# Contrast adjustment: rows of 48 KB in 4 buffers and 8 tiles in place of rows of 32 KB in 6 buffers and 12 tiles

## The chip, the cores and the metric

The kernel runs on one core of one Trainium2 chip. A core has a matrix engine (PE), a vector engine (DVE), a scalar engine (ACT), GpSimd (POOL) and SyncE (SP), 16 DMA engines that move data between HBM and the on-chip memory SBUF, and a small accumulation memory, PSUM, that PE writes. SBUF has 128 partitions; a tile is a block of all 128 partitions with so many elements in each. The metric is the device time of one execution, in microseconds (us).

## The reference

```python
def setup_inputs():
    batch, c, h, w = 16, 3, 512, 512
    return {
        "x": np.random.rand(batch, c, h, w).astype(np.float32),
        "factor": np.float32(1.5),
    }

def reference(x: np.ndarray, factor: np.float32) -> np.ndarray:
    mean = np.mean(x, axis=(2, 3), keepdims=True)
    return np.clip(mean + factor * (x - mean), 0, 1).astype(np.float32)
```

There are 48 images (batch times channel) of 262,144 pixels in float32. Each is read once, 50.33 MB in all, its mean is taken, and 1.5 times the pixel minus half the mean, cut to 0 and 1, is written, another 50.33 MB. A pixel can be written only when the whole of its image has been read.

## The kernel before

The input is seen as one flat row of numbers. A tile takes 128 rows of 8192 numbers (32 KB each, 4 MB together), one row for each partition. An image is 32 rows, so a tile holds four whole images, and each partition belongs to one image. There are 12 tiles.

The tiles pass through `ring` (L66), one SBUF tile of six slots; tile t uses slot t modulo 6. Everything is done in place in the slot. The instructions are issued in the order in which they are written out (the schedule is manual), so each engine's queue has them in this order; waits are put in from the data that they share.

- `load` (L68 to L76) issues on SP's queue. Tile 0 comes in two pieces, 2048 numbers of each row and then 6144; tile 1 alone; tiles 2 and 3 in one DMA, and tiles 4 and 5 in one, so that both tiles of a pair arrive together. The load of tile t + 6 is written after the compute of tile t, and waits for the store of tile t.
- `compute` (L78) sums each row. DVE takes 4352 of its numbers (L81), ACT the other 3840 with a copy whose sum is kept (L84; the copy goes into `junk` and is not used). Two matmuls with the constant matrix `blockw` (L86, L87) add the sums of the 32 partitions of each image and scale them, so that PSUM's `bias` holds the shift of its image for each partition.
- DVE then multiplies by the factor and adds the shift (L91) and clamps (L94), over the whole row at once; in tile 0 first over 2048 numbers and then over 6144.
- `store` (L100, L101) issues on ACT's queue after the clamp: tile 0 in two pieces, the others whole. So ACT's queue is: sum of tile t, store of tile t, sum of tile t + 1, and so on.

`blockw` is made by POOL at the start with five memsets (L61, L63).

Of the kernel before, what the change touches and what calls it, by code (L numbers as in the profile page):

```python
# [1 line left out]

# [4 lines left out]


P = 128  # L10
ROW = 8192
BUFS = 6
SHORT = 2048
FIRST = (SHORT, ROW - SHORT)
SUM = 4352


@with_exitstack
def kernel(
    ctx: ExitStack,  # L20
    tc: tile.TileContext,
    x: bass.AP,
    factor: float,
    out: bass.AP,
):

    nc = tc.nc
    f32 = mybir.dt.float32  # L30
    Alu = mybir.AluOpType
    Act = mybir.ActivationFunctionType

    B, C, H, W = x.shape
    n_img, n_pix = B * C, H * W
    ppi = n_pix // ROW
    per_tile = P // ppi
    n_tiles = n_img // per_tile
    assert ppi * ROW == n_pix and per_tile * n_tiles == n_img

    factor = float(factor)
    wconst = (1.0 - factor) / float(n_pix)

    x_f = x.rearrange("b c h w -> (b c h w)")
    out_f = out.rearrange("b c h w -> (b c h w)")

    def dram(ap, t, c0=0, c1=ROW):
        return bass.AP(tensor=ap.tensor, offset=t * P * ROW + c0, ap=[[ROW, P], [1, c1 - c0]])

    consts = ctx.enter_context(tc.tile_pool(name="consts", bufs=1))  # L50
    xpool = ctx.enter_context(tc.tile_pool(name="xpool", bufs=1))
    small = ctx.enter_context(tc.tile_pool(name="small", bufs=1))
    psum = ctx.enter_context(tc.tile_pool(name="psum", bufs=1, space=bass.MemoryType.PSUM))


    sums = small.tile([P, 2 * n_tiles], f32, name="sums")
    junk = small.tile([P, ROW - SUM], f32, name="junk")
    bias = psum.tile([P, n_tiles], f32, name="bias")

    blockw = consts.tile([P, P], f32, name="blockw")  # L60
    nc.gpsimd.memset(blockw, 0.0)  # L61
    for a in range(0, P, ppi):
        nc.gpsimd.memset(blockw[a : a + ppi, a : a + ppi], wconst)  # L63


    ring = xpool.tile([P, BUFS, ROW], f32, name="ring")  # L66

    def load(t, c0=0, c1=ROW, n=1):  # L68

        b = t % BUFS  # L70
        src = bass.AP(
            tensor=x_f.tensor,
            offset=t * P * ROW + c0,
            ap=[[ROW, P], [P * ROW, n], [1, c1 - c0]],
        )
        nc.sync.dma_start(out=ring[:, b : b + n, c0:c1], in_=src)  # L76

    def compute(t):  # L78
        xt = ring[:, t % BUFS, :]
        own = sums[:, 2 * t : 2 * t + 2]  # L80
        nc.vector.tensor_reduce(  # L81
            out=own[:, 0:1], in_=xt[:, 0:SUM], axis=mybir.AxisListType.X, op=Alu.add
        )
        nc.scalar.activation(out=junk, in_=xt[:, SUM:ROW], func=Act.Copy, accum_out=own[:, 1:2])  # L84
        shift = bias[:, t : t + 1]
        nc.tensor.matmul(shift, blockw, own[:, 1:2], start=True, stop=False)  # L86
        nc.tensor.matmul(shift, blockw, own[:, 0:1], start=False, stop=True)  # L87
        c = 0
        for n in FIRST if t == 0 else [ROW]:
            part = xt[:, c : c + n]  # L90
            nc.vector.tensor_scalar(  # L91
                out=part, in0=part, scalar1=factor, scalar2=shift, op0=Alu.mult, op1=Alu.add
            )
            nc.vector.tensor_scalar(  # L94
                out=part, in0=part, scalar1=0.0, scalar2=1.0, op0=Alu.max, op1=Alu.min
            )
            store(t, c, c + n)
            c += n

    def store(t, c0, c1):  # L100
        nc.scalar.dma_start(out=dram(out_f, t, c0, c1), in_=ring[:, t % BUFS, c0:c1])  # L101

    with tc.manual_schedule():
        load(0, c1=SHORT)
        load(0, c0=SHORT)
        load(1)
        load(2, n=2)
        load(4, n=2)
        for t in range(n_tiles):
            compute(t)  # L110
            if t + BUFS < n_tiles:
                load(t + BUFS)


# [1 line left out]
_INS = ['x', 'factor']  # L116
_OUTS = [((16, 3, 512, 512), 'float32')]

_NUMBERS = {'factor': 1.5}


# [26 lines left out]
```

## Time and profile before

| what | value |
|---|---|
| median of 4 runs | 239.38 us (239.18 to 239.67) |
| the profiled execution, whole | 239.2 us |
| its span, first to last instruction | 237.3 us |
| moved by DMA | 100.66 MB, 424 GB/s over the span |
| DVE busy | 163.1 us, 69% |
| ACT busy | 43.2 us, 18% |
| PE busy | 14.0 us, 6% |
| DMA packets | 3712 |

How to read it: the page describes one execution. The span is cut into 40 equal slices, each about 5.9 us; a digit in them is the busy share in tenths, and 9 is 90% or more. A line for a queue has its packets, its megabytes, and the time of its packets as a share of what 16 engines have in the span. A line for a group of instructions has the source line, engine, operation, output and inputs with their shapes (partitions x elements of each), how many there were, their busy time in us, the mean of one in ns, and then the idle time of the engine just before them with what ended most of it. A line of the timeline has the start in us, the duration in us, the engine, line and operation, and in brackets the idle time before it and what ended it. "ACTq" and "SPq" are the queues on which DMAs are issued; such a line tells of the issue, not of the transfer. Beside these views the trace has a record of each DMA packet: its queue, size, start and duration.

### The profile page before, as it was taken

The page shows a single profiled execution, that of the slowest core. Times are in us where ns is not written, and L with a number is a line of the kernel's source. Part 1 is how long each engine was busy: PE and PEld are TensorE (multiplying, and loading weights), DVE is VectorE, ACT ScalarE, POOL GpSimd, SP SyncE. Part 2 cuts the span into 40 slices and gives each one's busy share as a digit, 9 for nine tenths or more (in the row PEclk, how much of TensorE's full clock was granted, in tenths as well). Part 3 has the DMA queues.
Part 4 walks back from the last instruction along what each step waited for, and adds up shares of the span by engine and source line. Part 5 has one row for each costly group of instructions (what it writes and reads, how often), then busy time and mean ns, then how long its engine had stood idle before and what let it go on. Part 6 is the DMA issues. An engine that isn't in the chain of part 4 may idle for free.

```text
span 237.3 us, 285 instructions
## 1 busy us (share of the span) xinstructions
PE 14.0 (6%) x48; PEld 12.0 (5%) x48; DVE 163.1 (69%) x38; ACT 43.2 (18%) x25; POOL 0.9 (0%) x9
## 2 busy tenths in 40 slices
PE   0010010001010001010010100100100100010000
PEld 0010010001010001000010100100100100010000
DVE  0079989048989328998989898891892795687000
ACT  2050220041050023050320504101400500500000
POOL 1000000000000000000000000000000000000000
DMA  8999999999999999999999999999999999999996
GB/s 309 398 442 442 435 425 356 447 443 434 431 425 414 431 442 442 442 442 442 425 414 425 425 431 442 442 442 442 442 431 409 420 431 436 436 442 442 442 442 265
DMA packets 3712, 100.66 MB, mean 424 GB/s; under 512 B 384, under 2 KB 384, under 8 KB 384
## 3 DMA queue, kind: packets, MB, share of 16 engines
q1 hardware_dynamic: 1840, 50.33, 49.8%
q10 hardware_dynamic: 1872, 50.33, 49.1%
HBM read 50.33 MB, written 50.33 MB: 424 GB/s over the span
## 4 chain that ended last, share of the span: by engine, by line
DMA 57%; DVE 29%; another core or an unknown queue 3%; PE 1%; SPq 1%; issue 0%; DVEq 0%
DMA ring<-in_x_dram 41%; DMA out_dram<-ring 16%; DVE sums L81 10%; DVE ring L91 9%; DVE ring L94 9%; PE bias L87 1%; SPq L76 1%; DVEq L91 0%
## 5 line engine op out<-in xcount | busy, mean ns | idle before, releaser
L81 DVE TENSOR_REDUCE sums<-ring 128x1 f32<-128x4352 f32 x12 | 56.2, 4683 | 45.8 <-DMA ring<-in_x_dram 45.8
L84 ACT ACTIVATE junk<-ring 128x3840 f32<-128x3840 f32 x12 | 40.8, 3403 | 163.4 <-DMA ring<-in_x_dram 107.6
L91 DVE TENSOR_SCALAR ring<-ring,bias 128x8192 f32<-128x8192 f32 (+2 forms) x13 | 54.1, 4163 | 8.9 <-PE bias L87 7.4
L94 DVE TENSOR_SCALAR ring<-ring 128x8192 f32<-128x8192 f32 (+2 forms) x13 | 53.3, 4099 | 0.4
L86 PE MATMUL bias<-sums,blockw 128*128 128x1 f32 x24 | 7.0, 361 | 190.9 <-ACT junk L84 190.9
L86 PEld LDWEIGHTS bias<-sums,blockw 128*128 128x128 f32 x24 | 6.0, 311 | 191.8 <-ACT junk L84 175.5
L87 PE MATMUL bias<-sums,blockw 128*128 128x1 f32 x24 | 7.0, 362 | 4.3 <-DVE sums L81 3.9
L87 PEld LDWEIGHTS bias<-sums,blockw 128*128 128x128 f32 x24 | 6.0, 311 | 5.3 <-DVE sums L81 5.1
L84 ACT ACTIVATION_READ_ACCUMULATOR junk<-ring 128x1 f32 x12 | 2.2, 187 | 0.0
L84 ACT ACT_TABLE_LOAD x1 | 1.3, 1283 | 0.7 <-PEq L129 0.7
L63 POOL MEMSET blockw<- 32x32 f32 x4 | 0.5, 117 | 0.2
L61 POOL MEMSET blockw<- 128x128 f32 x1 | 0.2, 204 | 0.3 <-POOLq L129 0.3
L129 POOL MEMSET const-bfloat16-1.0<- 128x1 bf16 x1 | 0.1, 111 | 0.0
L129 POOL MEMSET const-uint8-127<- 128x1 uint8 x1 | 0.1, 111 | 0.0
L129 POOL MEMSET const-float32-1.0<- 128x1 f32 x1 | 0.1, 108 | 0.0
L129 POOL MEMSET const-float32-0.0<- 128x1 f32 x1 | 0.1, 103 | 0.2 <-issue 0.2
## 6 DMA issues: line engine op xcount, KB each, us to landing
out_dram<-ring ACTq DMA_DIRECT2D x11, 4096.0 KB, 36.0
ring<-in_x_dram SPq DMA_DIRECT2D x7, 4096.0 KB, 49.5
ring<-in_x_dram SPq DMA_DIRECT2D x2, 8192.0 KB, 66.8
ring<-in_x_dram SPq DMA_DIRECT2D x1, 3072.0 KB, 11.5
out_dram<-ring ACTq DMA_DIRECT2D x1, 3072.0 KB, 28.7
ring<-in_x_dram SPq DMA_DIRECT2D x1, 1024.0 KB, 4.6
out_dram<-ring ACTq DMA_DIRECT2D x1, 1024.0 KB, 18.5
```

Source lines behind the costliest of these rows:

```text
L61: nc.gpsimd.memset(blockw, 0.0)
L63: nc.gpsimd.memset(blockw[a : a + ppi, a : a + ppi], wconst)
L76: nc.sync.dma_start(out=ring[:, b : b + n, c0:c1], in_=src)
L81: nc.vector.tensor_reduce(out=own[:, 0:1], in_=xt[:, 0:SUM], axis=mybir.AxisListType.X, op=Alu.add)
L84: nc.scalar.activation(out=junk, in_=xt[:, SUM:ROW], func=Act.Copy, accum_out=own[:, 1:2])
L86: nc.tensor.matmul(shift, blockw, own[:, 1:2], start=True, stop=False)
L87: nc.tensor.matmul(shift, blockw, own[:, 0:1], start=False, stop=True)
L91: nc.vector.tensor_scalar(out=part, in0=part, scalar1=factor, scalar2=shift, op0=Alu.mult, op1=Alu.add)
L94: nc.vector.tensor_scalar(out=part, in0=part, scalar1=0.0, scalar2=1.0, op0=Alu.max, op1=Alu.min)
L129: nc = _bacc.Bacc("TRN2", target_bir_lowering=False, num_devices=1)
```

## The change

The rows become 12288 numbers, three parts of 4096 (48 KB), so a tile has 6 MB and six images, and there are 8 tiles. The ring has 4 slots in place of 6; it takes the same room. An image is 64 parts, which is 21 rows and a third, so image boundaries fall inside rows, at thirds: each row is in one image or in two, and its thirds have to be summed and shifted apart.

- `load` and `store` keep their queues. Tile 0 comes in with 2048 numbers of each row and then 10240; tile 1 alone; tiles 2 and 3 in one DMA; the others when their slot's store is done.
- Sums: DVE sums the first 6144 numbers as three halves of parts, in one instruction with three results (L129). ACT sums 2048 and then 4096 numbers, two copies written over their own input (L135). A row has five partial sums.
- POOL multiplies the five sums with `cls`, constant masks that say to which of three classes of images a third belongs, and gets 15 numbers (L136). One matmul with a new `blockw` adds them over the partitions (L142). DVE multiplies the result, three times over, with `pick`, constant masks again (L143), and reduces it to three shifts for each partition, one for each third (L149), which lie in SBUF.
- Shift: in tiles 1 to 6 DVE shifts the first third (L165) and ACT the other two (L155); in tiles 0 and 7 DVE takes two thirds and ACT one. The clamp is DVE's (L170), over the whole row of 12288; in tile 0 over 2048 and then 10240. It waits for DVE's and ACT's shifts.
- `of`, `cls`, `pick` and `blockw` are made by POOL at the start: two memsets, twelve affine selects, one addition and three copies; before the first select the program has the load of a POOL library.

On each queue the order is: SP has the loads only. ACT has, for a tile, its two sums, its shifts, the store. DVE has the reduce, the two small operations for the bias, its shifts, the clamp. POOL has its setup, and then one multiplication for each tile.

```diff
-ROW = 8192
-BUFS = 6
-SHORT = 2048
-FIRST = (SHORT, ROW - SHORT)
-SUM = 4352
+PART = 4096
+ROW = 3 * PART
+HALF = PART // 2
+BUFS = 4
+FIRST = (HALF, ROW - HALF)
+HEAD = (HALF, ROW - HALF)
+IMGS = 6
+CLS = 3
+NSUM = 5
...
+    of = consts.tile([P, IMGS, NSUM], f32, name="of")
+    pool.memset(of, 1.0)
...
+    cls = consts.tile([P, CLS, NSUM], f32, name="cls")
+    pool.tensor_tensor(out=cls, in0=of[:, 0:CLS], in1=of[:, CLS:IMGS], op=Alu.add)
+    pick = consts.tile([P, 3, CLS, NSUM], f32, name="pick")
+    for k in range(3):
+        pool.tensor_copy(
+            out=pick[:, k], in_=cls[:, :, 2 * k : 2 * k + 1].to_broadcast([P, CLS, NSUM])
+        )
...
-    nc.gpsimd.memset(blockw, 0.0)
-    for a in range(0, P, ppi):
-        nc.gpsimd.memset(blockw[a : a + ppi, a : a + ppi], wconst)
+    pool.memset(blockw, wconst)
...
+    while p0 < period:
...
+        pool.affine_select(
+            out=cols, in_=cols, pattern=[[-3 * period, P // period], [0, p1 - p0]],
+            compare_op=Alu.is_ge, fill=0.0, base=2 - units * first, channel_multiplier=3,
+        )
+        pool.affine_select(
+            out=cols, in_=cols, pattern=[[3 * period, P // period], [0, p1 - p0]],
+            compare_op=Alu.is_gt, fill=0.0, base=units * (last + 1), channel_multiplier=-3,
+        )
...
     def compute(t):
         xt = ring[:, t % BUFS, :]
-        own = sums[:, 2 * t : 2 * t + 2]
+        own = sums[:, t, :]
         nc.vector.tensor_reduce(
-            out=own[:, 0:1], in_=xt[:, 0:SUM], axis=mybir.AxisListType.X, op=Alu.add
-        )
-        nc.scalar.activation(out=junk, in_=xt[:, SUM:ROW], func=Act.Copy, accum_out=own[:, 1:2])
-        shift = bias[:, t : t + 1]
-        nc.tensor.matmul(shift, blockw, own[:, 1:2], start=True, stop=False)
-        nc.tensor.matmul(shift, blockw, own[:, 0:1], start=False, stop=True)
+            out=own[:, 0:3], in_=xt[:, 0 : 3 * HALF].rearrange("p (m c) -> p m c", m=3), axis=X,
+            op=Alu.add,
+        )
+        for m, a, b in (3, 3 * HALF, 4 * HALF), (4, 2 * PART, ROW):
+            part = xt[:, a:b]
+            nc.scalar.activation(out=part, in_=part, func=Act.Copy, accum_out=own[:, m : m + 1])
+        pool.tensor_tensor(
+            out=spread[:, t, :].rearrange("p (r m) -> p r m", r=CLS),
+            in0=own[:, None, :].to_broadcast([P, CLS, NSUM]),
+            in1=cls,
+            op=Alu.mult,
+        )
+        nc.tensor.matmul(totals[:, t, :], blockw, spread[:, t, :], start=True, stop=True)
+        nc.vector.tensor_tensor(
+            out=picked[:, t],
+            in0=totals[:, t, :][:, None, :].to_broadcast([P, 3, CLS * NSUM]),
+            in1=pick.rearrange("p k r m -> p k (r m)"),
+            op=Alu.mult,
+        )
+        nc.vector.tensor_reduce(out=bias[:, t, :], in_=picked[:, t], axis=X, op=Alu.add)
+        kd = 1 if 0 < t < n_tiles - 1 else 2
+        for k in range(kd, 3):
+            third = xt[:, k * PART : (k + 1) * PART]
+            nc.scalar.activation(
+                out=third, in_=third, func=Act.Identity, scale=factor, bias=bias[:, t, k : k + 1]
+            )
         c = 0
         for n in FIRST if t == 0 else [ROW]:
-            part = xt[:, c : c + n]
-            nc.vector.tensor_scalar(
-                out=part, in0=part, scalar1=factor, scalar2=shift, op0=Alu.mult, op1=Alu.add
-            )
+            end = c + n
+            for k in range(kd):
+                a, b = max(c, k * PART), min(end, (k + 1) * PART)
+                if a < b:
+                    part = xt[:, a:b]
+                    nc.vector.tensor_scalar(
+                        out=part, in0=part, scalar1=factor, scalar2=bias[:, t, k : k + 1],
+                        op0=Alu.mult, op1=Alu.add,
+                    )
+            part = xt[:, c:end]
             nc.vector.tensor_scalar(
                 out=part, in0=part, scalar1=0.0, scalar2=1.0, op0=Alu.max, op1=Alu.min
             )
-            store(t, c, c + n)
+            store(t, c, end)
+            c = end
...
-        load(0, c1=SHORT)
-        load(0, c0=SHORT)
+        c = 0
+        for n in HEAD:
+            load(0, c, c + n)
+            c += n
         load(1)
         load(2, n=2)
-        load(4, n=2)
         for t in range(n_tiles):
             compute(t)
             if t + BUFS < n_tiles:
                 load(t + BUFS)
```

## The prediction

> **What bounds the kernel now.** I read the slices of the span first, then the DMA queues, then the groups of instructions, and last the timeline around the last tile.
>
> ```profile
> DMA  8999999999999999999999999999999999999996
> GB/s 309 398 442 442 435 425 356 447 443 434 431 425 414 431 442 442 442 442 442 425 414 425 425 431 442 442 442 442 442 431 409 420 431 436 436 442 442 442 442 265
> DMA packets 3712, 100.66 MB, mean 424 GB/s; under 512 B 384, under 2 KB 384, under 8 KB 384
> q1 hardware_dynamic: 1840, 50.33, 49.8%
> q10 hardware_dynamic: 1872, 50.33, 49.1%
> ```
>
> The DMA engines are at 9 tenths or more from the second slice to the last but one, and the two queues' packets fill 49.8 + 49.1 = 98.9% of 16 engines' span, 234.7 of 237.3 us. The kernel is bound by DMA from end to end. 384 packets under 512 B are the completion writes: 16 for each of 24 DMAs. The other 3328 are rows, 208 on each engine.
>
> ```profile
> L81 DVE TENSOR_REDUCE sums<-ring 128x1 f32<-128x4352 f32 x12 | 56.2, 4683 | 45.8 <-DMA ring<-in_x_dram 45.8
> L84 ACT ACTIVATE junk<-ring 128x3840 f32<-128x3840 f32 x12 | 40.8, 3403 | 163.4 <-DMA ring<-in_x_dram 107.6
> L86 PE MATMUL bias<-sums,blockw 128*128 128x1 f32 x24 | 7.0, 361 | 190.9 <-ACT junk L84 190.9
> L84 ACT ACTIVATION_READ_ACCUMULATOR junk<-ring 128x1 f32 x12 | 2.2, 187 | 0.0
> L61 POOL MEMSET blockw<- 128x128 f32 x1 | 0.2, 204 | 0.3 <-POOLq L129 0.3
> ```
>
> These give the prices of compute. The idle time of DVE and ACT is put down to loads, that of PE to ACT's sums.
>
> ```profile
> 18.14 1.29 DVE L91 TENSOR_SCALAR ring<-ring,bias 128x2048 f32<-128x2048 f32 x1 [0.68 <-PE bias L87]
> 203.85 4.69 DVE L81 TENSOR_REDUCE sums<-ring 128x1 f32<-128x4352 f32 x1 [4.99 <-DMA ring<-in_x_dram]
> 209.27 4.49 DVE L91 TENSOR_SCALAR ring<-ring,bias 128x8192 f32<-128x8192 f32 x1 [0.74 <-PE bias L87]
> 213.80 4.43 DVE L94 TENSOR_SCALAR ring<-ring 128x8192 f32<-128x8192 f32 x1
> 218.26 0.34 ACTq L101 DMA_DIRECT2D out_dram<-ring  x1
> ```
>
> The last tile is in at 203.8 and its store is issued at 218.26. By the packet records of the trace the store ahead of it ends only at 226.5, and the last store's first packet starts at 225.9: the last tile's compute has 7.7 us to spare, and is no tail. So only two things can change the time: what the packets themselves cost, and whether DMA goes idle.
>
> **Part 1, the packets.** Bytes stay 100.66 MB. A packet is one row of one DMA. The packet records of undisturbed stores give 309 ns for 8 KB, 912 ns for 24 KB, 1213 ns for 32 KB: a line of 0.03678 ns per byte plus 8 ns per packet. Before, per engine and direction: 8 x 0.309 + 8 x 0.912 + 88 x 1.213 = 116.5 us, twice 233.0, and 24 completion writes of 9 ns, 0.2. The records run from 1.74 to 236.17 us, 234.4, so 1.2 us is lost: 0.8 in the first load (8 packets in 3.25 us for 2.47), 0.4 elsewhere. After: 8 tiles, the first in two pieces, give 8 packets of 8 KB, 8 of 40 KB at 1.514, 56 of 48 KB at 1.816, each extrapolated on the line: 116.3, twice 232.55, and 17 DMAs (8 loads, 9 stores) with 0.15. That is 0.55 us less; the 1.2 us lost stay, since the first piece is 8 KB a row again. Nothing in the trace is as long as 48 KB. Bounds: no saving per byte over the 32 KB row, 1.5 x 1.213 = 1.82, leaves 0.1 us of gain; if long loads go at the mean of all 32 KB loads, 1225 ns instead of 1213, the 56 loads cost 56 x 1.5 x 0.012 = 1.0 more, and the change loses 0.5. I take the line, because three sizes lie on it within 1 ns and most of the load excess stands between 21 and 40 us, when stores begin.
>
> The Trainium skill, "SBUF — State Buffer", section "The DMA setup-cost knee", gives every transfer some 2 us that don't scale with bytes and advises the largest single transfers. As a sum, 7 DMAs fewer would be 14 us of gain, some 225 us. The queue rows leave no place for it: 24 such costs are 48 us and 2.6 us of the span are without packets, since one queue moves data while the other's transfer completes.
>
> **Part 2, compute of a tile.** L81 is 4352 / 4.68; at 0.96 elements per ns and 0.15 fixed, 6144 elements take 6.55. ACT's sums: 3840 in 3.40 is 1.2 per ns and 0.2 fixed, so 2048 and 4096 take 1.9 + 3.6, and two accumulator reads 0.4: 5.9, beside DVE's 6.55 and shorter, so it hides there; were ACT held back, each 0.6 us beyond counts. Clamp and shift go by 0.521 ns per element plus 0.2 (1.29 for 2048, 4.49 for 8192): 4096 is 2.35, 12288 is 6.6. The bias: before, sums to shift is 0.75 (two passes of the second matmul, 0.6, and hops). After, a POOL multiply of 15 elements, the matmul, a DVE multiply of 45 and a DVE reduce to 3. No row shows such small ones; the nearest are POOL memsets of 0.1 to 0.2 and accumulator reads of 0.19. From 1.1 (each at 0.1) to 3 (POOL and both DVE operations at 0.5 and more); I take 1.5, near the memsets. The second matmul of a tile goes away, 0.6 us that was hidden beside DVE's reduce. That ACT's copies are written over the ring instead of junk, and that the shift reads its bias from SBUF, not PSUM, I cost at nothing: as many elements are written, and L91 with the PSUM operand takes 4.49 where L94 without takes 4.43. Then ACT shifts two thirds, 2 x 3.6 + 0.1 = 7.3, with DVE's one third (2.35) beside it, and the clamp 6.6 waits for ACT. DVE per middle tile: 6.55 + 1.5 + 7.3 + 6.6 = 22; the last tile, where DVE takes two thirds, 6.55 + 1.5 + 4.7 + 6.6 = 19.5. One tile's DMA, in and out, is 16 x 1.816 = 29.05, so compute is 76% of it (before 14.4 of 19.4, 74%). On ACT's queue the store stands behind the shifts and waits for the clamp, and the next tile's ACT sums stand behind the store; they begin with DVE's reduce, as before. SP's queue holds loads alone, each waiting for the store that frees its slot.
>
> **Part 3, does DMA go idle?** Tile 0: its rows end at 5.0 + 8 x 1.514 = 17.1, DVE starts 0.5 later as before, reduce to 24.2, bias at 25.7. ACT's third to 29.3 holds the first store to 29.4 (before 20.7); the second, after DVE's 1.2, 2.35 and a clamp of 5.5, goes at 37.3. Tile 1 is in by 32, its store goes at 59.3. Loads run alone until then, and are covered: the four slots hold 25.2 MB, as six did. Tiles 2 and 3 are one DMA and arrive together: 17.1 + 24 x 1.816 plus the store packets between them (8 x 0.309, some 7 x 1.514) is about 73. The second store ends near 75, and frees the slot of tile 4; the load queue is empty for some 4 us while the store queue runs alone. From 76.5 each load takes 29.05 beside a store: tile 6 is in at 164, tile 7 at 193. Compute follows: tile 2 from 73, 3 from 95, 4 from 117, 5 from 139, 6 on arrival, its store at 186; tile 7 to 193 + 19.5 = 212.5. DMA ends at 236.2 - 0.55 = 235.6, the last store takes 8 x 1.816 = 14.5 alone and must go by about 220. Spare: 7 us, nearly that of before. Nothing is late, so the path stays DMA and compute is costed at nothing: its cover is the store backlog.
>
> **Part 4, POOL's setup.** Before: 5 memsets on blockw, done by 1.6 us. After, 2 memsets, 12 affine selects in chains of two, one add, three copies, and a library load ahead of the selects. It is wanted at 24.2. Bounds from the memset rows: 18 x 0.2 = 3.6 us at the least; if each select were as slow as a 4683 ns reduce, 12 x 4.7 = 56. I take under 20 us, nearest to the memsets by size (42 columns or fewer). A delay X of tile 0 costs nothing at first: loads of 58 us and the first tile's stores of 14.6 us keep DMA busy to 74 while tile 1's store would go at 59.3 + X. Beyond X = 14, setup past 38 us, DMA stands still.
>
> The Trainium skill, "GPSIMD Engine Reference", section "Instruction dispatch", adds about 6 us for the first call of a freshly loaded library. With it the setup is 10 to 26 us, still inside the 38; no row before shows such a load.
>
> **The sum.** The profiled execution took 239.2 (span 237.3, 1.9 around it); less 0.55 is 238.65. The median of the four runs is 0.18 above the profiled one: 239.38 - 0.55 = 238.8.
>
> **Rivals.** A, compute becomes the bound and it is slower: tiles 2 to 7 run back to back from 73: 73 + 5 x 22 + 19.5 = 202.5 against 220, so 17.5 / 6 = 2.9 us more per tile is free; beyond it every 1 us per tile is 6 us of tail. At 26 us a tile (POOL hop and small DVE operations 5.5 instead of 1.5) it loses 6.6: 245. For it: four hops over three engines that no row prices; against: all small rows are near 0.2. B, the POOL setup comes after 38 us: at 44 DMA idles 6 us, 245. For it: twelve selects unknown; against: the small sizes. C, long rows do not pay: 0.1 of gain to 0.5 of loss, 239.3 to 239.9. For it: 8 ns a packet is all the gain there is; against: the line of three sizes.
>
> **How the numbers follow.** A measurement here can tell 0.2%, 0.48 us, from no change: the bar is 238.9. My case has 0.68 with 238.2 to 239.2; below, the other 0.4 us of loss and the 0.2 by which runs lay under their median also come off; above, half the gain stays. Of it 0.52 is faster, 0.16 the same. A has 0.10 and B 0.07, all slower. C has 0.15: 0.02 faster, 0.06 same, 0.07 slower. Sums: 0.54, 0.22, 0.24. The range takes C whole and the small end of A and B, to 241; some 0.15 lies above, 0.05 below.
>
> **What would show it.** 2576 packets, 272 of them small; 48 KB packets at 1816 ns (part 1; at 1820 and more C); DMA digits of 9 to the last slice; middle clamps of 6.6 starting 15.4 us after their reduce (part 2); the last store issued near 212 (part 3; past 220 is A); tile 0's matmul at 25 (part 4; past 39 is B). The forecast fails if the digits of DMA fall anywhere before the end, or if time around the span grows from 1.9, for instance with the library.

## The result, and the profile after

The changed kernel takes 239.65 us (median of 35 executions, 239.19 to 245.19) beside 239.26 us for the kernel before (54 executions, 238.97 to 239.91): a ratio of 1.0025, 95% interval 1.0014 to 1.0036. It is slower by a quarter of a per cent, where 0.25% faster was forecast. The ratio is one of means of fast executions: it leaves out the four from 244.6 to 245.2, as any that is more than 1.5% above the fastest of its kernel (their granted clock is 1.0 as in the others), and the median of the other 31 is 239.50. The shape of the numbers matters more than the median: 23 of the 35 are between 239.19 and 239.93, near the kernel before, and 12 are above 240. No execution of the kernel before is above 240. The execution profiled here took 240.18, with a span of 238.1.

The slices of the span and the DMA queues of the changed kernel:

```profile
DMA  7999989998999999999999999999999999999994
GB/s 286 440 462 396 454 376 447 462 383 388 484 410 427 405 512 405 396 479 446 396 396 520 405 396 471 454 396 396 520 396 405 471 447 396 405 512 405 405 446 215
DMA packets 2577, 100.67 MB, mean 423 GB/s; under 512 B 272, under 2 KB 272, under 8 KB 272
q1 hardware_dynamic: 1280, 50.33, 49.6%
q10 hardware_dynamic: 1296, 50.33, 48.8%
```

The packets are as counted in the prediction (2576 and one instruction fetch), and nowhere before the last slice does DMA stand still. The share of the packets, 98.4% of 238.1, is 234.3 us, 0.4 less than before. At the end only the last slice is different: 4 tenths where it was 6.

Its groups of instructions, and POOL's setup and the last tile in the timeline:

```profile
L129 DVE TENSOR_REDUCE sums<-ring 128x3 f32<-128x6144 f32 x8 | 52.4, 6550 | 45.8 <-DMA ring<-in_x_dram 45.8
L155 ACT ACTIVATE ring<-ring,bias 128x4096 f32<-128x4096 f32 x14 | 51.3, 3704 | 18.3 <-DVE bias L149 18.3
L143 DVE TENSOR_TENSOR picked<-totals,pick 128x45 f32<-128x45 f32 x8 | 1.6, 205 | 8.5 <-PE totals L142 8.5
L136 POOL TENSOR_TENSOR spread<-sums,cls 128x15 f32<-128x15 f32 x8 | 1.7, 214 | 198.6 <-DVE sums L129 198.6
L149 DVE TENSOR_REDUCE bias<-picked 128x3 f32<-128x45 f32 x8 | 1.6, 200 | 0.3
```

```profile
1.10 0.27 POOL L70 TENSOR_SCALAR_AFFINE_SELECT of<-of 128x30 f32<-128x30 f32 x1
3.55 0.47 POOL L81 COPY pick<-cls 128x15 f32<-128x15 f32 x3
...
204.13 0.21 POOL L136 TENSOR_TENSOR spread<-sums,cls 128x15 f32<-128x15 f32 x1 [29.23 <-DVE sums L129]
...
205.52 4.62 DVE L165 TENSOR_SCALAR ring<-ring,bias 128x4096 f32<-128x4096 f32 x2
...
210.24 6.56 DVE L170 TENSOR_SCALAR ring<-ring 128x12288 f32<-128x12288 f32 x1
216.83 0.34 ACTq L124 DMA_DIRECT2D out_dram<-ring  x1
```

Compute is what the prediction said it would be, each small operation 0.2 us, POOL ready at 4 us. The last store is issued at 216.8, and by the packet records its first packet starts at 221.1: 4.3 us to spare. So neither compute nor the setup is the answer, and the answer lies in the DMA packets.

**One account for all traces.** The packet records let the end of DMA be written as a sum, in us for one engine (the mean of 16): the start of the first packet, plus what the packets take by their sizes (8 ns each and 0.03678 ns per byte), plus what single packets took beyond that (held up), less the time in which the records of neighbouring packets overlap. To that comes how far the last of the 16 engines ends after their mean. The records do not name the engine; each DMA has 16 completion writes, one behind the last packet of each engine, and an engine's end is read from these. For the kernel before and for all traces of the changed kernel that follow:

| traced execution | time | first packet | by size | held up | overlap | mean end | last engine after the mean |
|---|---|---|---|---|---|---|---|
| before | 239.2 | 1.94 | 233.0 | 1.58 | 0.65 | 235.93 | 0.24 |
| after | 240.18 | 1.99 | 232.5 | 1.73 | 0.41 | 235.91 | 1.02 |
| after, second trace | 239.51 | 1.95 | 232.5 | 1.77 | 0.41 | 235.92 | 0.57 |
| after, third | 239.34 | 2.00 | 232.5 | 1.70 | 0.41 | 235.90 | 0.22 |
| after, fourth | 242.62 | 2.02 | 232.5 | 1.92 | 0.41 | 236.13 | 3.20 |
| after, fifth | 239.40 | 2.00 | 232.5 | 1.59 | 0.41 | 235.79 | 0.31 |
| after, sixth | 240.39 | 2.01 | 232.5 | 1.80 | 0.41 | 235.99 | 1.36 |
| after, seventh | 239.31 | 1.98 | 232.5 | 1.67 | 0.41 | 235.82 | 0.25 |

Each line closes to 0.1 us (232.5 is 232.55 rounded). Two things stand in it. The 0.5 us by size are there, but 0.24 of them come back because fewer packets overlap (0.65 over 208 packets and 0.41 over 144 are both some 3 ns each), and about 0.15 because more is held up (1.74 on the mean of the seven, 1.68 on that of the four quiet ones). The mean end moves by 0.15 us at most in the quiet executions. And the three traced executions above 240 are those in which one or two engines end late.

### The profile page after: what moved, and what is told of

The parts are those of the page before. It is cut to its first block, busy times and chain, and to the rows that moved or that the text cites. A ratio compares the mean times of both kernels' runs of the same rounds, so it can differ in the third digit from the quotient of the medians.

```text
span 238.1 us, 250 instructions
## 1 busy us (share of the span) xinstructions
PE 4.9 (2%) x16; PEld 4.0 (2%) x16; DVE 131.4 (55%) x44; ACT 97.4 (41%) x47; POOL 5.0 (2%) x30
## 4 chain that ended last, share of the span: by engine, by line
DMA 40%; DVE 32%; ACT 8%; another core or an unknown queue 7%; issue 2%; PE 1%; POOL 0%; SPq 0%; POOLq 0%; DVEq 0%; ACTq 0%
DMA ring<-in_x_dram 22%; DMA out_dram<-ring 17%; DVE ring L170 14%; DVE sums L129 14%; ACT ring L155 8%; DVE ring L165 4%; PE totals L142 1%; DVE picked L143 0%; DVE bias L149 0%; POOL spread L136 0%; SPq L120 0%; POOLq L217 0%; POOLq L136 0%; ACTq L155 0%
## 5 line engine op out<-in xcount | busy, mean ns | idle before, releaser
L135 ACT ACTIVATE ring<-ring 128x2048 f32<-128x2048 f32 (+1 forms) x16 | 44.1, 2756 | 92.8 <-DMA ring<-in_x_dram 63.4
L129 DVE TENSOR_REDUCE sums<-ring 128x3 f32<-128x6144 f32 x8 | 52.4, 6550 | 45.8 <-DMA ring<-in_x_dram 45.8
L170 DVE TENSOR_SCALAR ring<-ring 128x12288 f32<-128x12288 f32 (+2 forms) x9 | 52.6, 5849 | 30.5 <-ACT ring L155 30.3
L155 ACT ACTIVATE ring<-ring,bias 128x4096 f32<-128x4096 f32 x14 | 51.3, 3704 | 18.3 <-DVE bias L149 18.3
L165 DVE TENSOR_SCALAR ring<-ring,bias 128x4096 f32<-128x4096 f32 (+1 forms) x11 | 23.6, 2158 | 0.3
L142 PE MATMUL totals<-spread,blockw 128*128 128x15 f32 x16 | 4.9, 383 | 200.1 <-POOL spread L136 200.1
L142 PEld LDWEIGHTS totals<-spread,blockw 128*128 128x128 f32 x16 | 4.0, 310 | 200.9 <-POOL spread L136 200.9
L143 DVE TENSOR_TENSOR picked<-totals,pick 128x45 f32<-128x45 f32 x8 | 1.6, 205 | 8.5 <-PE totals L142 8.5
L136 POOL TENSOR_TENSOR spread<-sums,cls 128x15 f32<-128x15 f32 x8 | 1.7, 214 | 198.6 <-DVE sums L129 198.6
L135 ACT ACTIVATION_READ_ACCUMULATOR ring<-ring 128x1 f32 x16 | 3.0, 188 | 0.0
L149 DVE TENSOR_REDUCE bias<-picked 128x3 f32<-128x45 f32 x8 | 1.6, 200 | 0.3
L97 POOL TENSOR_SCALAR_AFFINE_SELECT blockw<-blockw 128x42 f32<-128x42 f32 (+2 forms) x5 | 0.9, 220 | 0.0
L101 POOL TENSOR_SCALAR_AFFINE_SELECT blockw<-blockw 128x42 f32<-128x42 f32 (+2 forms) x5 | 0.9, 220 | 0.0
```

The lines of the kernel that those rows point to most:

```text
L97: pool.affine_select(out=cols, in_=cols, pattern=[[-3 * period, P // period], [0, p1 - p0]], compare_op=Alu.is_ge, fill=0.0, base=2 - unit ...
L101: pool.affine_select(out=cols, in_=cols, pattern=[[3 * period, P // period], [0, p1 - p0]], compare_op=Alu.is_gt, fill=0.0, base=units * ( ...
L129: nc.vector.tensor_reduce(out=own[:, 0:3], in_=xt[:, 0 : 3 * HALF].rearrange("p (m c) -> p m c", m=3), axis=X, op=Alu.add,)
L135: nc.scalar.activation(out=part, in_=part, func=Act.Copy, accum_out=own[:, m : m + 1])
L136: pool.tensor_tensor(out=spread[:, t, :].rearrange("p (r m) -> p r m", r=CLS), in0=own[:, None, :].to_broadcast([P, CLS, NSUM]), in1=cls, ...
L142: nc.tensor.matmul(totals[:, t, :], blockw, spread[:, t, :], start=True, stop=True)
```

## The experiments

The runs are grouped by what they ask. In time, the four that traced the changed kernel once more came last of all. The theories have letters in the expectations: T, the last tile's compute is no longer covered; D, later L, engines fall behind with long packets.

### The changed kernel again, six times

No edit in these.

> The changed kernel as it is, for its spread on this chip and a second trace. Median near 239.65 us; of its executions some lie within 0.3 us of the kernel before and others 1 to 5 us above it. Theory T (tail): what is lost is the cover of the last tile. In the first trace the last store is issued at 216.8 us, only 4.3 us before the store ahead of it has moved its rows (before: 7.7), and executions in which the last load lands 5 us or more later leave DMA idle at the end. By T a slow trace shows the packets of the last store starting after a hole. Theory D (engine lag): one of the 16 DMA engines falls behind with 48 KB rows; in the first trace one engine ends 0.8 us after the other fifteen. By D a slow trace shows no hole, and one or a few engines that end late.

> The changed kernel as it is, a third time, for more executions and another trace. Median 239.4 to 239.7; two to four of twelve above 240. If the traced execution is one of them, by L one or some of the engines end late and the rest within 0.3 us of 235.9; by T the last store's packets start after a hole.

> The changed kernel once more, one traced execution. About one execution in three is above 240 us. If this one is: by theory L the mean end of the 16 engines' last packets is within 0.3 us of 235.9 to 236.5 and some engines end 1 us or more after it, after load packets that took longer; by theory T (tail cover) the 16 engines end together, and the last store's packets start after a hole of the length by which the execution is late.

> As the run before it, one more traced execution of the changed kernel.

> As the two runs before it, one more traced execution of the changed kernel.

> As the three runs before it, one more traced execution of the changed kernel.

Measured: the first 239.48 (12 executions, 239.07 to 241.18; ratio 1.0015, 1.0003 to 1.0028); the next 239.57 (12, 239.30 to 241.52; 1.0036, 1.0015 to 1.0056); the four single ones 242.62, 239.40, 240.39 and 239.31. With the first 35, 20 of 63 executions of the changed kernel are above 240. The first of these runs was on another chip than the other five, and late executions came on both.

The slices of the late one, 242.62, and its last tile in the timeline; then both of the quiet one, 239.40:

```profile
DMA  7999998999999999999999999999999999999990
GB/s 283 436 458 392 523 411 343 444 392 452 398 480 414 458 392 433 482 392 401 507 401 392 507 401 392 515 401 392 507 392 401 490 418 401 458 450 401 433 474 25
```

```profile
212.62 6.56 DVE L170 TENSOR_SCALAR ring<-ring 128x12288 f32<-128x12288 f32 x1
219.21 0.34 ACTq L124 DMA_DIRECT2D out_dram<-ring  x1
```

```profile
DMA  7999999999989999999999999999999999999996
GB/s 287 442 464 398 422 406 453 464 370 403 486 353 486 398 489 439 398 398 522 406 398 456 472 398 398 489 439 398 398 522 406 398 449 480 398 398 480 447 398 265
```

```profile
209.77 6.56 DVE L170 TENSOR_SCALAR ring<-ring 128x12288 f32<-128x12288 f32 x1
216.36 0.34 ACTq L124 DMA_DIRECT2D out_dram<-ring  x1
```

In the late one DMA is at 9 tenths up to the last slice but one: no hole stands ahead of the last store. It is issued 2.9 us later, and still ahead of its first packet at 221.2, the same time as in the quiet one (221.1). But in the last slice 25 GB/s are moved, not 265. By the completion writes 14 of the 16 engines end between 235.7 and 236.2, as in a quiet execution, and the other two at 236.7 and 239.3. In the other late one the last two end at 236.7 and 237.4, the rest by 236.2. This is L, seen directly in the changed kernel, and T is out as the cause of these executions.

The records of the execution of 242.62 also show how one falls behind. The difference between the first and the last engine at the end of each load of one tile is 0.6 us in the load that ends at 109.4, 1.1 at 138.9, 2.1 at 168.9 and 3.6 at 199.5; the second-last engine ends that last load at 196.8, so it is one engine that lags. The packets that took longest stand at the beginning of those loads, which start at 110.6, 139.6 and 168.6: load packets at 111.2 (2.16 us in place of 1.82), 140.7 (2.62) and 170.7 (3.39). The lag roughly doubles from load to load, and what these packets take beyond 1.82 (0.3, 0.8 and 1.6) is most of what it grows by (0.5, 1.0 and 1.6).

### The last tile in two pieces

```diff
+LAST = (3 * HALF, 3 * HALF)
...
-        for n in FIRST if t == 0 else [ROW]:
+        for n in FIRST if t == 0 else LAST if t == n_tiles - 1 else [ROW]:
```

> The last tile is shifted, clamped and stored in two pieces of 6144 numbers, so that its first store is issued some 4 us earlier (about 212.5 against 216.8); all else is the changed kernel. T: the executions above 240 us go away, all but those that were 4 us late; median 239.2 to 239.3. D: no change, median about 239.6 with the same spread. Its last packets are 24 KB, which costs 0.1 us at most in packets.

Measured: 239.32 (11 executions, 239.15 to 242.71; ratio 1.0018, 0.9994 to 1.0041), with the first piece's store issued at 212.0. The median is where T had put it, but it can't be told from the unchanged kernel's 239.48 beside it, and an execution 3.4 us late is still there with 4.8 us more cover. By itself this was not conclusive; the traces above are.

### The transfers with the clamp alone, 48 KB and 32 KB rows

In both, `compute` is cut down to the clamp and the store; POOL's setup and the small tiles are gone.

```diff
     def compute(t):
         xt = ring[:, t % BUFS, :]
-        own = sums[:, t, :]
...
         c = 0
         for n in FIRST if t == 0 else [ROW]:
             end = c + n
-            for k in range(kd):
...
             part = xt[:, c:end]
             nc.vector.tensor_scalar(
                 out=part, in0=part, scalar1=0.0, scalar2=1.0, op0=Alu.max, op1=Alu.min
             )
             store(t, c, end)
```

> The changed kernel's loads and stores (48 KB rows, 4 slots, 8 tiles) with the sums, masks, matmul and shifts left out: only the clamp of DVE stands between load and store, 6.6 us a tile in place of 22. T: no spread, 238.9 to 239.1. D: the spread of the changed kernel is there, executions of 240 to 245 us among them. If the 0.55 us of the packet sum were real and only compute took it away, this is 0.5 us faster than the same with 32 KB rows.

> The loads and stores of the kernel before (32 KB rows, 6 slots, 12 tiles) with the sums, matmuls and shifts left out in the same way. T and D: 239.2, like the kernel before, since DMA was its bound. Against e3 it gives the price of the packets alone: 0.55 us by the packet sum as I put it; 0.3 us if it is counted that neighbouring packets overlap by some 3 ns in the records (8 - 3 = 5 ns for each of 64 packets).

Measured: 48 KB rows 244.03 (4 executions, 243.66 to 244.64; ratio 1.0201, 1.0187 to 1.0215), 32 KB rows 239.11 (11, 238.86 to 239.30; 0.9994, 0.9985 to 1.0002). Slices of the first and of the second:

```profile
DMA  7999989999999999999999999999999999999991
GB/s 282 455 390 477 368 382 442 477 393 496 390 390 398 455 406 439 455 406 398 471 431 390 471 439 382 463 439 398 463 406 423 463 423 415 463 423 415 463 423 81
```

```profile
DMA  8999899999999999999999999999999999999996
GB/s 305 355 441 458 375 464 428 430 441 441 425 425 419 436 425 441 441 441 430 441 441 419 419 430 425 436 441 441 436 436 441 425 430 419 425 430 441 441 441 265
```

With 15 us less compute for each tile the 48 KB rows are not at 239 but nearly 5 us above, in every execution, and again the last slice is nearly empty, 81 GB/s. T is refuted here: the last store is issued at 209.7, and its first packet starts at 222.5. In the account: held up 3.90 (32 KB: 1.55), mean end 237.96 (235.89), last engine 2.80 after the mean (0.46). The 16 engines end anywhere from 236.8 to 240.8. Besides the stall at the first stores (0.9 us of each engine at 27) packets are held up at 67 to 79, in the middle of the pair's load and of the store beside it (1.1 us of each engine), and the engines come apart there: the difference between first and last is 0.6 us at the end of the store before (55) and 2.3 at the end of that store (88); at the end of the kernel it is 4.0. The 32 KB rows without most of their compute are 0.13 us faster than the kernel before, which can't be told from no change.

### Cutting the packets, the slots, and the first pieces

```diff
+        cuts = [c0, c1] if c1 - c0 < ROW else [0, ROW // 2, ROW]
+        for a, e in zip(cuts, cuts[1:]):
-        nc.sync.dma_start(out=ring[:, b : b + n, c0:c1], in_=dram(x_f, t, c0, c1, n))
+            nc.sync.dma_start(out=ring[:, b : b + n, a:e], in_=dram(x_f, t, a, e, n))
```

and the same for the store. With the clamp alone:

> The clamp-only kernel with 48 KB rows (sums, masks, matmul and shifts left out; it took 244.0 us), with every whole load and store cut into two DMAs of half rows: same 4 slots, same 8 tiles, same bytes, but packets of 24 KB. Theory L (long packets: a 48 KB packet held up on some engines at a change of queue spreads the 16 engines): about 239.2 to 239.5, no engines that end late. Rival R (4 slots of 6 MB: fewer and larger pieces let a queue run empty): 243 to 245 as before.

Measured: 240.00 (10 executions, 239.67 to 240.60; ratio 1.0031, 1.0022 to 1.0040). With the same slots, tiles and bytes, packets of 24 KB take away 4 of the 4.9 us. This tells packet length from the ring: rival R had said 243 to 245. One thing goes with the length and is not told from it: the number of DMAs, 30 in place of 17. In the account: by size 233.4, held up 1.95, overlap 0.84, mean end 236.40, last engine 0.54 after it. It is 0.5 above the expected range, by the mean end and not by the spread: against the 32 KB rows the mean end is 0.5 later, 0.2 of it packets (after the overlap) and 0.4 held up, less 0.1 of an earlier start.

With all compute:

> The changed kernel with every whole load and store cut into two DMAs of half rows, 24 KB packets; compute is not touched, and both stores of a tile still follow the one clamp. L: the spread goes away: median 239.2 to 239.4, none above 240. R and T (tail cover): median 239.4 to 239.7, and of ten executions two or three above 240. 24 KB packets cost 64 more on each engine than 48 KB ones do, 0.3 us at 5 ns, the price of the kernel before or a little more.

Measured: 241.02 (6 executions, 240.51 to 241.37; ratio 1.0074, 1.0061 to 1.0086). The spread is small (0.9 from lowest to highest, last engine 0.42 after the mean), as L says; the time isn't. But six executions are few: with 20 late in 63, six without a late one would come by chance about once in ten (an estimate, 43/63 to the sixth power). The mean end is 237.02, 1.1 later than with 48 KB: packets 0.4 after the overlap, and 0.7 more held up, by a second stall at 136 to 139 of 0.6 us on each engine, after the load queue had been empty from 125.6 to 131.8. So short packets in this arrangement lose more than the spread costs.

```diff
-BUFS = 6
+BUFS = 4
...
-        load(4, n=2)
```

With 32 KB rows and the clamp alone:

> The clamp-only kernel with 32 KB rows and 12 tiles (239.1 us with 6 slots) with 4 slots only: 16 MB of ring in place of 24. Compute is the clamp alone, as there. L: 239.1, unchanged. R: slower, by 1 us or more.

Measured: 239.37 (10 executions, 238.85 to 245.82; ratio 1.0015, 0.9994 to 1.0036): eight between 238.85 and 239.73, one at 241.83, one at 245.82. The trace is of the 241.83: 15 engines end by 236.3, the other at 238.9. Expected by L was no change at all. Long packets are not the only way to a late engine; with fewer slots it is seen at 32 KB too, in two of ten.

With 32 KB rows and all compute of the kernel before:

> The kernel before, 32 KB rows and all of its compute, with 4 slots of 4 MB in place of 6. Theory L (48 KB packets alone): 239.2 to 239.3, no spread. Theory R2 (fewer slots alone make executions that end late; with clamp only and 4 slots of 32 KB rows two of ten were 2.5 and 6.5 us late): median within 0.4 of 239.3 and one to three of ten executions above 240.

Measured: 239.87 (11 executions, 239.30 to 240.81; ratio 1.0035, 1.0021 to 1.0048). It did not tell what it was made for: the median is later than R2 had it, and five of the eleven are above 240. The trace is of one of the others, 239.61. In it the engines end together (0.09 after the mean); the last store is issued at 225.7 and its packets start at 226.6, when the store before it has just ended on every engine: here T is at work, the cover of the last tile used up. So 4 slots cost this kernel 0.7 us, in the trace by another way than the changed kernel's. None of its executions above 240 was traced, so whether an engine lags in them stays open.

```diff
-FIRST = (HALF, ROW - HALF)
-HEAD = (HALF, ROW - HALF)
+FIRST = (ROW,)
+HEAD = (ROW,)
```

With the clamp alone and 48 KB rows:

> The clamp-only kernel with 48 KB rows, with tile 0 loaded, clamped and stored whole, so no packet of 8 KB or 40 KB is in it. If what spreads the engines is the short packets of the first store against the long ones of the loads (S), it falls from 244.0 to 239.5 or so; if it is the long packets at any change of queue (L), it stays at 243 to 245. By R it stays too.

Measured: 243.41 (4 executions, 243.08 to 246.03; ratio 1.0206, 1.0160 to 1.0252). The short packets are not what sets the engines apart.

The same for FIRST alone, in the changed kernel and in the kernel before:

> The changed kernel with tile 0 shifted, clamped and stored whole in place of 2048 and then 10240 numbers; it is still loaded in two pieces. In each trace of the changed kernel all 16 load packets in flight at 50.4 us, where the second store takes over from the first, take 2.7 to 2.9 us in place of 1.8: 1.0 us of DMA time. If that stall belongs to the change from one store to the next behind short packets (S1), it goes away, about 238.5 to 238.9. If a stall of this size comes with whichever store is first (S2, it is so in the clamp-only kernel with 48 KB rows and no pieces: 1.3 us), the median stays at 239.3 to 239.6. The spread of executions stays by theory L.

> The kernel before with tile 0 shifted, clamped and stored whole. Its load packets are held up by 0.3 us when the first store starts and by 0.7 when the second does. S1: 238.4 to 238.8, faster than both kernels. S2: 239.1 to 239.4.

Measured: the changed kernel 242.47 (6 executions, 240.82 to 246.61; ratio 1.0118, 1.0092 to 1.0144), the kernel before 240.50 (10, 239.44 to 241.76; 1.0055, 1.0038 to 1.0072). Both expectations are wrong, and so are both of their theories. The stall isn't saved: it moves to the start of the first store and is larger (1.5 us at 36 to 45, before 1.03 at 50; in the kernel before 1.4 at 28 to 34, before 1.0 in two places), and in the changed kernel another 0.9 us is held up from 54 to 70. And the first packets of the first store then start over 2.7 us from engine to engine, in both, where they start over 0.5 us (48 KB) and 1.4 us (32 KB) with a short first piece; at the end the last engine is 1.4 and 1.5 us after the mean. No run beat the kernel before with the full computation.

## Why the prediction was wrong

Two of its steps failed, and each takes roughly half of the miss. Part 1's gain of 0.55 us was worth about 0.1, which moves the forecast of 238.8 to some 239.3, where the quiet executions lie (the four traced ones took 239.31 to 239.51). The rest, up to the median of 239.65, is that part 3 let all 16 engines end together: the last one ends 0.2 to 3.2 us after the mean in the seven traces. Point by point, by its parts:

- **Part 1, the packets: the sizes were right, the sum was not.** 48 KB packets of stores take 1815 ns (1816 extrapolated), 40 KB 1514; by size 232.5 us for each engine (232.55). The term that was mis-sized is the 8 ns per packet: the records of neighbours overlap by 3, so 64 packets less save 0.26 and not 0.5. The 1.2 us "lost" that were to stay were a difference, what is held up less this overlap, and so they could not stay when packets became fewer. What is held up is itself 0.15 more on the mean of the seven traces.
- **Part 3, "does DMA go idle?": the step that turned a lost gain into a loss.** It followed one engine for all 16. DMA does not go idle, and the last store had its cover (4.3 us in place of 7: the pair of tiles came in at 75.4, not 73, and tile 7 at 197.4, not 193). But the end is that of the slowest engine: 20 of 63 executions are above 240, and in the three of these that were traced one or two engines lag. The prediction had taken the evenness of the engines before, 235.6 to 236.2, for granted; with 48 KB packets it is no longer given. The range held the median; the direction was wrong.
- **Part 2, compute: right**, row by row: reduce 6.55, ACT's two shifts 7.31 (7.3), clamp 6.56 (6.6), the bias from the end of the reduce 1.5. One detail differs: ACT issues tile 0's first store at 28.5 while its shift runs to 29.7; I had it wait for the shift.
- **Part 4, POOL's setup: right**, near its lower bound: ready at 4.0 us. The first select starts 0.04 us after the memset of `blockw` ends, and the time around the span is 1.8 to 2.1 us in the seven traces, 1.9 before. The 6 us that the Trainium skill ("GPSIMD Engine Reference", "Instruction dispatch") gives for the first call to a freshly loaded kernel of this engine don't show here.
- **The rivals.** A (compute) and B (setup) did not come. C named the outcome, 239.3 to 239.9, and "long rows do not pay", but its reason, a higher price for every long packet, is not what happens: the mean of the 48 KB loads is 1836 ns, 21 above the stores, and most of that is one stall at 50 us.

What is shown and what is not: that late engines end the late executions is shown in the traces of 240.18, 240.39 and 242.62 (none above 243 was traced). That packet length, with the number of DMAs that goes with it, sets them apart in this ring is shown with the clamp alone (244.0 against 240.0, same slots, tiles and bytes). For the changed kernel with all its compute the same cause is argued, not shown: 24 KB packets gave an even end there, but in six executions, and with 4 slots of 32 KB rows executions above 240 come too. Why a lagging engine is held up more at the beginning of each load, and why some executions are spared, stays open; that a restart out of step feeds the lag is a reading of the trace, and no run takes the restarts away.

## What to carry to other kernels

When DMA is busy from end to end, a longer row saves only the cost per packet that doesn't overlap, here 5 ns, so 64 packets on each engine were worth some 0.3 us. The end of such a kernel is that of its slowest DMA engine: look at the last slice and at the last packets of all engines, and compare many executions, since the median hides a third that are late. Changes to the start of a stream (how the first store joins the loads) moved these kernels by 1 to 3 us (240.50 for 239.20, 242.47 for 239.57), more than all the packets that could be saved.

## What had not been expected of the hardware

- One DMA engine's lag can grow through a kernel: 0.6, 1.1, 2.1, 3.6 us at the ends of four loads in a row, while fourteen of the sixteen engines end within 0.5 us of each other.
- Loads in flight are held up where stores begin or one store follows the first: by 0.8 to 1.5 us on the mean of the engines, in all kernels here. In the three pairs of kernels that differ in it, it is less with a short first piece of 8 KB rows: 1.0 for 1.4, 1.0 for 1.5 and, with the clamp alone, 0.9 for 1.3.
- Less compute made the same transfers slower: 48 KB rows with the clamp alone take 244.0, with all compute 239.5 to 239.65.
